# Where the low parts of streamed weights are made: VectorE's subtraction, or a negative from ScalarE and an adding DMA

## The chip, the cores and the metric

The kernel runs on one core of a Trainium2 chip. The metric is the time of the device, in microseconds (us), of one execution: the median of three executions of the kernel before is 1641.2 us (1640.48 to 1641.28).

The engines are named as the profile names them: PE is TensorE's matmul, PEld its weight load, DVE is VectorE, ACT is ScalarE, POOL is GpSimd, SP is SyncE. ACTq, POOLq and SPq are the queues from which these engines issue DMAs.

## The reference

The reference is a chain of two blocks on a sequence of 512 tokens with 1024 features, in float32. The first block projects the normed input by `w_in`, attends in chunks, convolves, gates and projects back. The second block has a layer with a sparse attention and a gated linear attention, a layer with stick-breaking attention, and behind each an MLP of width 4096. Nearly all of the arithmetic is the product of activations with weight matrices:

```
proj = jnp.einsum('bsd,de->bse', h, w_in[l])
...
def squared_relu_mlp(n, w_up, w_down):
    return jnp.square(jax.nn.relu(n @ w_up)) @ w_down
...
for layer in range(DEPTH_2):
    n = rmsnorm_2(h, g_mix[layer])
    ...
    h = h + squared_relu_mlp(rmsnorm_2(h, g_ffn[layer]), w_up[layer], w_down[layer])
```

## The kernel before

**Three products for one.** TensorE multiplies in a format that keeps fewer bits than float32 (float32r in the code). So every operand is split: `hi` is the value as that format keeps it, `lo` is what is left, and a product is made of three matmuls: hi by hi, lo by hi, hi by lo. For activations `split` makes the two parts, for weights that stream in from memory `split_w` (L161).

**A piece of weights.** The weights come through SyncE's queue into `raw` tiles (two buffers, 1 MB each as a rule, `load_raw`, L174). Half of a raw tile is a piece: 128 partitions by 1024 elements. For a piece `split_w` has ScalarE write `whi` as a copy (L170) and VectorE write `wlo` as raw minus whi (L171). `whi` and `wlo` have three buffers each, so a piece can be made while TensorE still uses the two before it. Both instructions are put ahead of other work by `first()`, a priority for the scheduler that orders each engine's queue.

**Who uses pieces.** `proj_fm` (L251) streams a matrix as 1024 rows by 128 columns, so its pieces are 128x8x128 (for matrices with 512 or 256 rows the columns grow); one piece serves one or two tiles of 512 tokens, 24 matmuls in all: per row block hi by hi (L246), lo by hi (L247), hi by lo (L248). The last matmul that reads a `whi` buffer is an L247, the last that reads a `wlo` an L248. `proj_tok` (L268) streams pieces of 128x2x512, also 24 matmuls (L282 to L284). There are 214 pieces. In the program 128 of the 208 that the change touches are 128x8x128, 20 are 128x4x256 and 60 are 128x2x512.

**Around them.** Attention runs beside the projections as generators (`weave`, `tick`), a step behind every few matmuls. In an MLP, eight pieces of `w_up` (six, and two of the next quarter) alternate with four calls of `down_pair`, which take their weights apart in another way (`weight_forms`, L1143): its own `put` stays as it is, and it uses the same three buffers of `whi` and `wlo`. GpSimd issues no DMA in this kernel; it adds squares (`SumSq`, L308), rotates queries and keys (`rope`, L645 to L647), and forms parts of the gated linear attention (`level`, L875 to L881). The order on each engine is the scheduler's; every engine takes its queue in order.

Of the kernel before, what the change touches and what calls it, by code (L numbers as in the profile page):

```python
# [8 lines left out]
F32 = mybir.dt.float32  # L9
# [3 lines left out]
AF = mybir.ActivationFunctionType  # L13
ALU = mybir.AluOpType
AX = mybir.AxisListType

P = 128
# [26 lines left out]
def body(tc, A, out, dbg=None):  # L44
    nc = tc.nc
    ACT, DVE, PE, POOL = nc.scalar, nc.vector, nc.tensor, nc.gpsimd

    with ExitStack() as es:
# [12 lines left out]
        def uid(s):  # L61
            cnt[0] += 1
            return f"{s}_{cnt[0]}"
# [94 lines left out]
            PE.matmul(ps, q[0], k[1], start=False, stop=False)  # L158
            PE.matmul(ps, q[1], k[0], start=False, stop=True)

        def split_w(raw, w, pieces=1):  # L161

            kd = raw.shape[1]
            hi = wp.tile([P, kd, w], F32R, tag="whi", bufs=3, name=uid("whi"))
            lo = wp.tile([P, kd, w], F32R, tag="wlo", bufs=3, name=uid("wlo"))
            n = kd // pieces
            for k in range(0, kd, n):
                ks = slice(k, k + n)
                with first():
                    ACT.activation(hi[:, ks, :], raw[:, ks, :], AF.Copy)  # L170
                    DVE.tensor_tensor(lo[:, ks, :], raw[:, ks, :], hi[:, ks, :].bitcast(F32), op=ALU.subtract)  # L171
            return hi, lo

        def load_raw(kd, w, *parts, pieces=1):  # L174
# [79 lines left out]
        def proj_fm(W, r0, c0, ncols, xs, evac):  # L254


            kd = len(xs)
            w = 1024 // kd
            for ch in range(0, ncols, 2 * w):
                cw = min(2 * w, ncols - ch)  # L260
                raw = load_raw(kd, cw, (0, W[r0:r0 + kd * P, c0 + ch:c0 + ch + cw]))
                for hf in range(0, cw, w):
                    hi, lo = split_w(raw[:, :, hf:hf + w], w)
                    for mt in range(0, w, P):
                        fm_tile(hi, lo, mt, xs, evac, (ch + hf + mt) // P)
                        yield

        def proj_tok(W, r0, c0, xs, evac, tts=range(NT), pieces=1):  # L268

            kd = len(xs)  # L270
            pss = {tt: psum("tk") for tt in tts}
            for k0 in range(0, kd, 4):
                raw = load_raw(4, 512, (0, W[r0 + k0 * P:r0 + (k0 + 4) * P, c0:c0 + 512]), pieces=pieces)
                for k2 in range(0, 4, 2):
                    hi, lo = split_w(raw[:, k2:k2 + 2, :], 512, 2 if pieces > 1 and k0 + k2 == 0 else 1)
                    for j in range(2):
                        k = k0 + k2 + j
                        for tt in tts:
                            xh = xs[k][0][:, tt * P:(tt + 1) * P]
                            xl = xs[k][1][:, tt * P:(tt + 1) * P]  # L280
                            ps = pss[tt]
                            PE.matmul(ps, xh, hi[:, j, :], start=k == 0, stop=False)  # L282
                            PE.matmul(ps, xh, lo[:, j, :], start=False, stop=False)  # L283
                            last = PE.matmul(ps, xl, hi[:, j, :], start=False, stop=k == kd - 1)  # L284
                            tick(last)
                    run_pending(last)
                    if k < kd - 1:
                        yield
            for tt in tts:
                with first():  # L290
                    evac(tt, pss[tt])
            yield
# [55 lines left out]
        r0 = cp.tile([P, NT], F32, name="r0")  # L348
# [39 lines left out]
        W = A["w_in"]  # L388
# [246 lines left out]
        W = A["w_in_ab"]  # L635
# [38 lines left out]
        raw = load_raw(KD, P, (0, W[:, 2048:2176]), (96, W[:, 3144:3160]))  # L674
# [597 lines left out]
        W = A["w_in_c"]  # L1272
# [171 lines left out]
```

## Time and profile before

| what | us |
|---|---|
| median of three executions | 1641.2 |
| the profiled execution | 1639.93 |
| its span, first to last instruction | 1638.2 |
| PE busy | 1601.4 |
| DVE busy | 1040.7 |
| ACT busy | 732.9 |
| POOL busy | 207.8 |

A matmul's record lasts longer than the step from one matmul to the next, since matmuls are pipelined: the step is read from the start times in the timeline, not from the mean of a group. Times are counted from the start of the span.

### The profile page before, as it was taken

Reading aid. Unit: us, or ns where it says so; the run is one execution under the profiler, and the core shown is the slowest. Engines: PE = TensorE matmul, PEld = TensorE weight load, DVE = VectorE, ACT = ScalarE, POOL = GpSimd, SP = SyncE. Lnnn points to the kernel's source line nnn. Section 1 sums busy time; section 2 is a strip of 40 time slices with the busy share of each in tenths; the row PEclk is TensorE's granted clock in tenths of the full one; section 3 lists DMA queues with packets and bytes.
Section 4 is the critical chain, followed back from the end, with each engine's and each line's share of the span. In section 5 each row is a group of like instructions: output and inputs, shape, how many; then the busy total and the mean of one; then the engine's idle time right before and its main releaser. Section 6 shows DMA issues by size and latency. Waiting matters only on the chain.

```text
span 1638.2 us, 21483 instructions
## 1 busy us (share of the span) xinstructions
PE 1601.4 (98%) x8440; PEld 1358.3 (83%) x8440; DVE 1040.7 (64%) x1887; ACT 732.9 (45%) x1172; POOL 207.8 (13%) x295
## 2 busy tenths in 40 slices
PE   9999999999998889999999999999999999999999
PEld 7887888888777667888989898888887789898987
DVE  5546443444658886568678795434557876877952
ACT  6343332225544535455554443334554554535341
POOL 3100000003322451210000000211213200000000
PEclk9999999999999999999999999999999999999999
DMA  6421123233222110223333322332121233333322
GB/s 203 150 77 52 52 77 118 88 104 115 79 78 77 52 52 26 71 85 103 104 103 104 103 89 92 103 99 82 52 78 52 77 103 104 103 104 103 104 77 77
DMA packets 129220, 146.39 MB, mean 89 GB/s; under 512 B 4048, under 2 KB 109152, under 8 KB 129120
## 3 DMA queue, kind: packets, MB, share of 16 engines
q1 hardware_dynamic: 122848, 141.11, 26.4%
q10 hardware_dynamic: 6272, 3.92, 0.8%
q8 instruction: 66, 1.08, 0.3%
q14 instruction: 34, 0.28, 0.0%
HBM read 142.92 MB, written 2.10 MB: 89 GB/s over the span
## 4 chain that ended last, share of the span: by engine, by line
PE 90%; DVE 4%; POOL 2%; ACT 1%; issue 1%; DMA 0%; POOLq 0%; DVEq 0%
PE fm L246 16%; PE fm L248 16%; PE fm L247 16%; PE tk L282 5%; PE tk L283 5%; PE tk L284 5%; PE sw L1195 5%; PE sw L1194 5%; PE sw L1193 5%; PE tr L331 3%; PE oc L1342 1%; PE S L1318 1%; PE S L469 1%; PE pa L493 1%; DVE wlo L171 1%
## 5 line engine op out<-in xcount | busy, mean ns | idle before, releaser
L246 PE MATMUL fm<-hi,whi 128*128 128x512 f32 x1224 | 484.2, 396 | 0.0
L247 PE MATMUL fm<-lo,whi 128*128 128x512 f32 x1224 | 477.5, 390 | 0.7 <-DVE lo L152 0.7
L248 PE MATMUL fm<-hi,wlo 128*128 128x512 f32 x1224 | 477.7, 390 | 0.0
L170 ACT ACTIVATE whi<-raw 128x1024 fp32r<-128x1024 f32 (+1 forms) x214 | 225.9, 1056 | 441.6 <-PE fm L247 286.8
L171 DVE TENSOR_TENSOR wlo<-raw,whi 128x1024 fp32r<-128x1024 f32 (+1 forms) x214 | 270.5, 1265 | 198.9 <-ACT whi L170 198.1
L248 PEld LDWEIGHTS fm<-hi,wlo 128*128 128x128 f32 x1224 | 229.8, 188 | 48.3
L247 PEld LDWEIGHTS fm<-lo,whi 128*128 128x128 f32 x1224 | 230.1, 188 | 47.8 <-DVE lo L152 2.0
L246 PEld LDWEIGHTS fm<-hi,whi 128*128 128x128 f32 x1224 | 230.0, 188 | 45.7 <-issue 0.5
L282 PE MATMUL tk<-whi,hi 128*128 128x512 f32 x472 | 196.6, 416 | 1.2 <-ACT va L795 0.6
L284 PE MATMUL tk<-whi,lo 128*128 128x512 f32 x472 | 187.3, 397 | 0.0
L283 PE MATMUL tk<-wlo,hi 128*128 128x512 f32 x472 | 186.8, 396 | 0.0
L308 POOL TENSOR_TENSOR ssq<-ssq,sq 128x512 f32<-128x512 f32 x25 | 38.6, 1553 | 557.6 <-ACT sq L306 557.3
L1195 PE MATMUL sw<-hi,wlo 128*128 128x256 f32 x384 | 108.7, 283 | 0.0
L1194 PE MATMUL sw<-lo,whi 128*128 128x256 f32 x384 | 108.7, 283 | 0.0
L1193 PE MATMUL sw<-hi,whi 128*128 128x256 f32 x384 | 108.6, 283 | 0.0
L284 PEld LDWEIGHTS tk<-whi,lo 128*128 128x128 f32 x472 | 89.9, 191 | 19.4
L282 PEld LDWEIGHTS tk<-whi,hi 128*128 128x128 f32 x472 | 90.8, 192 | 18.3 <-ACT vb L795 1.5
L283 PEld LDWEIGHTS tk<-wlo,hi 128*128 128x128 f32 x472 | 90.6, 192 | 15.5 <-DVE wlo L171 0.2
L1193 PE MATMUL sw<-hi,wh 128*128 128x256 f32 x288 | 81.5, 283 | 0.0
L1194 PE MATMUL sw<-lo,wh 128*128 128x256 f32 x288 | 81.5, 283 | 0.0
L1195 PE MATMUL sw<-hi,wl 128*128 128x256 f32 x288 | 81.5, 283 | 0.0
L1194 PEld LDWEIGHTS sw<-lo,whi 128*128 128x128 f32 x384 | 73.7, 192 | 0.2
(353 smaller groups left out, 2338.2 us busy)
## 6 DMA issues: line engine op xcount, KB each, us to landing
raw<-in_w_up SPq DMA_DIRECT2D x32, 1024.0 KB, 5.3
raw<-in_w_down SPq DMA_DIRECT2D x32, 1024.0 KB, 4.9
raw<-in_w_in SPq DMA_DIRECT2D x22, 1024.0 KB, 5.0
raw<-in_w_in_ab SPq DMA_DIRECT2D x14, 1024.0 KB, 4.9
raw<-in_w_in_c SPq DMA_DIRECT2D x12, 1024.0 KB, 4.9
raw<-in_w_out SPq DMA_DIRECT2D x4, 1024.0 KB, 5.0
raw<-in_w_out_ab SPq DMA_DIRECT2D x4, 1024.0 KB, 5.0
raw<-in_w_out_c SPq DMA_DIRECT2D x4, 1024.0 KB, 4.9
```

The source lines that it names most:

```text
L170: ACT.activation(hi[:, ks, :], raw[:, ks, :], AF.Copy)
L171: DVE.tensor_tensor(lo[:, ks, :], raw[:, ks, :], hi[:, ks, :].bitcast(F32), op=ALU.subtract)
L246: PE.matmul(ps, wh, xh, start=k == 0, stop=False)
L247: PE.matmul(ps, wh, xl, start=False, stop=False)
L248: last = PE.matmul(ps, wl, xh, start=False, stop=k == kd - 1)
L282: PE.matmul(ps, xh, hi[:, j, :], start=k == 0, stop=False)
L283: PE.matmul(ps, xh, lo[:, j, :], start=False, stop=False)
L284: last = PE.matmul(ps, xl, hi[:, j, :], start=False, stop=k == kd - 1)
L331: PE.transpose(ps[:, j * P:(j + 1) * P], s_, ident)
L1193: PE.matmul(half(ps, n % 2), wh, xh, start=j == 0, stop=False)
L1194: PE.matmul(half(ps, n % 2), wh, xl, start=False, stop=False)
L1195: last = PE.matmul(half(ps, n % 2), wl, xh, start=False, stop=j == 3)
```

## The change

For the pieces of `proj_fm`, and for those of `proj_tok` but its first call (which loads in four parts), VectorE's subtraction is left out. ScalarE writes `wlo` as the negative of `whi`, and GpSimd issues a DMA that adds the weights, read once more from memory, to `wlo` in place. `src` is the view of the matrix that the piece holds. The constant at the end is the number of bytes in each partition that are set aside for GpSimd's DMAs.

```diff
-        def split_w(raw, w, pieces=1):
+        def split_w(raw, w, pieces=1, src=None):
...
                 with first():
                     ACT.activation(hi[:, ks, :], raw[:, ks, :], AF.Copy)
-                    DVE.tensor_tensor(lo[:, ks, :], raw[:, ks, :], hi[:, ks, :].bitcast(F32), op=ALU.subtract)
+                    if src is None:
+                        DVE.tensor_tensor(lo[:, ks, :], raw[:, ks, :], hi[:, ks, :].bitcast(F32), op=ALU.subtract)
+                    else:
+                        ACT.activation(lo[:, ks, :], hi[:, ks, :].bitcast(F32), AF.Copy, scale=-1.0)
+                        nc.gpsimd.dma_start(lo[:, ks, :], src, accum_op=ALU.add)
...
                 for hf in range(0, cw, w):
-                    hi, lo = split_w(raw[:, :, hf:hf + w], w)
+                    src = W[r0:r0 + kd * P, c0 + ch + hf:c0 + ch + hf + w].rearrange("(k p) c -> p k c", p=P)
+                    hi, lo = split_w(raw[:, :, hf:hf + w], w, src=src)
...
                 for k2 in range(0, 4, 2):
-                    hi, lo = split_w(raw[:, k2:k2 + 2, :], 512, 2 if pieces > 1 and k0 + k2 == 0 else 1)
+                    ks_ = r0 + (k0 + k2) * P
+                    src = None if pieces > 1 else W[ks_:ks_ + 2 * P, c0:c0 + 512].rearrange("(k p) c -> p k c", p=P)
+                    hi, lo = split_w(raw[:, k2:k2 + 2, :], 512, 2 if pieces > 1 and k0 + k2 == 0 else 1, src)
...
-    nc = bacc.Bacc("TRN2", target_bir_lowering=False, num_devices=1, dynamic_dma_scratch_size=2048)
+    nc = bacc.Bacc("TRN2", target_bir_lowering=False, num_devices=1, dynamic_dma_scratch_size=4096)
```

The scheduler orders the queues anew. ScalarE's queue in the first quarter of the first MLP, before (`ha` is the hidden activation of a tile, `t3b` a scale made once):

```order
L170 ACTIVATE whi_6153<-raw_6151 128x1024
L324 ACTIVATE t3b_6035<-bc_6030 128x512
L1117 ACTIVATE ha_6037<-ha_6037 128x512
L1136 ACTIVATE hi_6049<-ha_6037 128x256
L1117 ACTIVATE ha_6040<-ha_6040 128x512
L148 ACTIVATE hi_6061<-ha_6040 128x512
```

and after, at the same place:

```order
L171 ACTIVATE whi_6253<-raw_6251 128x1024
L332 ACTIVATE t3b_6133<-bc_6128 128x512
L175 ACTIVATE wlo_6254<-whi_6253 128x1024
L1125 ACTIVATE ha_6135<-ha_6135 128x512
L1125 ACTIVATE ha_6138<-ha_6138 128x512
L1144 ACTIVATE hi_6147<-ha_6135 128x256
L148 ACTIVATE hi_6159<-ha_6138 128x512
```

The negative (L175) stands one place behind the copy here, with other work between the two; elsewhere it follows the copy directly. GpSimd's queue there before, where the sums of squares ahead of the first MLP are followed at once by those behind it:

```order
L308 TENSOR_TENSOR ssq_5761<-ssq_5761,sq_5851 128x512
L308 TENSOR_TENSOR ssq_5761<-ssq_5761,sq_5878 128x512
L308 TENSOR_TENSOR ssq_5761<-ssq_5761,sq_5899 128x512
L308 TENSOR_TENSOR ssq_8841<-ssq_8841,sq_8913 128x512
L308 TENSOR_TENSOR ssq_8841<-ssq_8841,sq_8952 128x512
```

and after:

```order
L176 DMA wlo_6049<-in_w_up 128x8x128
L316 TENSOR_TENSOR ssq_5853<-ssq_5853,sq_5973 128x512
L316 TENSOR_TENSOR ssq_5853<-ssq_5853,sq_5994 128x512
L176 DMA wlo_6099<-in_w_up 128x8x128
L176 DMA wlo_6166<-in_w_up 128x8x128
L176 DMA wlo_6199<-in_w_up 128x8x128
L176 DMA wlo_6254<-in_w_up 128x8x128
L176 DMA wlo_6287<-in_w_up 128x8x128
```

Where nothing stood, the 40 DMAs of this MLP now stand in a row. GpSimd's queue in the attention of the second block, where it rotates the queries, before:

```order
L875 TENSOR_TENSOR dl_4557<-Bc_3498 128x512
L878 TENSOR_TENSOR dl_4557<-dl_4557,kb_3685 128x128x2
L875 TENSOR_TENSOR dl_4610<-Bc_3566 128x512
L645 TENSOR_TENSOR rp_4342<-qa_4304,ropeQ 128x128
L646 TENSOR_TENSOR rp_4343<-qa_4304,ropeQ 128x128
L647 TENSOR_TENSOR qa_4304<-rp_4342,rp_4343 128x4x32
```

and after:

```order
L883 TENSOR_TENSOR dl_4636<-Bc_3563 128x512
L176 DMA wlo_4654<-in_w_in_ab 128x2x512
L886 TENSOR_TENSOR dl_4636<-dl_4636,kb_3752 128x128x2
L883 TENSOR_TENSOR dl_4690<-Bc_3631 128x512
L653 TENSOR_TENSOR rp_4418<-qa_4380,ropeQ 128x128
L654 TENSOR_TENSOR rp_4419<-qa_4380,ropeQ 128x128
L176 DMA wlo_4737<-in_w_in_ab 128x2x512
L655 TENSOR_TENSOR qa_4380<-rp_4418,rp_4419 128x4x32
```

Two DMAs have come in between, one of them between two steps of a rotation.

## Rows read from the trace of the kernel before

**Rows 1.** The page's first part: busy us, share of the span, instructions
```profile
PE 1601.4 (98%) x8440; PEld 1358.3 (83%) x8440; DVE 1040.7 (64%) x1887; ACT 732.9 (45%) x1172; POOL 207.8 (13%) x295
```
**Rows 2.** Costliest groups: instruction, count, busy us, mean ns, idle before it by releaser
```profile
L170 ACT ACTIVATE whi<-raw 128x1024 fp32r<-128x1024 f32 (+1 forms) x214 | 225.9, 1056 | 441.6 <-PE fm L247 286.8
L171 DVE TENSOR_TENSOR wlo<-raw,whi 128x1024 fp32r<-128x1024 f32 (+1 forms) x214 | 270.5, 1265 | 198.9 <-ACT whi L170 198.1
...
L308 POOL TENSOR_TENSOR ssq<-ssq,sq 128x512 f32<-128x512 f32 x25 | 38.6, 1553 | 557.6 <-ACT sq L306 557.3
```
**Rows 3.** Timeline in the second MLP: start, us, engine, instruction, idle before it
```profile
1402.83 1.06 ACT L170 ACTIVATE whi<-raw 128x1024 fp32r<-128x1024 f32 x1 [0.92 <-PE fm L247]
...
1403.80 0.62 ACT L1117 ACTIVATE ha<-ha 128x512 f32<-128x512 f32 x1
...
1403.93 1.23 DVE L171 TENSOR_TENSOR wlo<-raw,whi 128x1024 fp32r<-128x1024 f32 x1 [0.18 <-ACT whi L170]
...
1408.27 1.06 ACT L170 ACTIVATE whi<-raw 128x1024 fp32r<-128x1024 f32 x1 [3.40 <-PE fm L247]
```
**Rows 4.** Instructions of line L170 alone, by stretch: length, ACT busy (count), clock, DMA
```profile
33.00:77.00 44.00, 9.22 (x9) 1.00 0.55 169
77.00:191.00 114.00, 12.98 (x13) 1.00 0.18 58
191.00:412.00 221.00, 42.45 (x40) 1.00 0.31 98
```
**Rows 5.** Timeline, ScalarE alone, between two quarters of the first MLP
```profile
802.57 1.06 ACT L170 ACTIVATE whi<-raw 128x1024 fp32r<-128x1024 f32 x1 [0.26 <-PE sw L1194]
...
812.64 1.06 ACT L170 ACTIVATE whi<-raw 128x1024 fp32r<-128x1024 f32 x1 [0.72 <-PE sw L1194]
820.88 1.06 ACT L170 ACTIVATE whi<-raw 128x1024 fp32r<-128x1024 f32 x1 [6.66 <-PE fm L247]
```
**Rows 6.** DMA issues: count, KB each, median us from issue to landing
```profile
raw<-in_w_up SPq DMA_DIRECT2D x32, 1024.0 KB, 5.3
...
raw<-in_w_in_ab SPq DMA_DIRECT2D x1, 512.0 KB, 3.4
raw<-in_w_in_ab SPq DMA_DIRECT2D x1, 64.0 KB, 2.2
```
**Rows 7.** Instructions on the tile raw: ns min/median/max, first and last start
```profile
L171 DVE TENSOR_TENSOR wlo<-raw,whi x214: 691/1225/7231, 6.6 to 1619.3; 128x1024 fp32r<-128x1024 f32 x106, 128x512 fp32r<-128x512 f32 x1
L180 SPq DMA_DIRECT2D raw<-in_w_up x32: 367/368/368, 692.5 to 1551.0; - x32
```
**Rows 8.** Busy us by stretch: PE, PEld, DVE, ACT, POOL, granted clock, DMA share, GB/s
```profile
500.00:600.00 100.00, 84.00 (x394) 67.70 (x392) 89.49 (x192) 43.34 (x81) 50.79 (x64) 0.93 0.16 53
...
1300.00:1540.00 240.00, 240.00 (x1481) 217.03 (x1480) 185.78 (x300) 116.36 (x175) 0.00 (x0) 1.00 0.31 101
```
**Rows 9.** Chain that ended last, 500 to 620 us, shares by line
```profile
by line: DVE wlo L171 9.8%; DVE isc L786 8.2%; issue 7.1%; DVE m L785 6.7%; PE tk L282 5.7%; PE gr L887 5.7%; PE tk L283 5.2%; PE tk L284 5.2%; POOL rp L646 4.0%; POOL dl L875 3.6%; POOL dl L878 3.5%; POOL rp L645 2.9%; POOL qa L647 2.8%; P
```
**Rows 10.** PE's waits, 500 to 660 us: waiting line, releaser, us, times, longest
```profile
PE tr L331 <- POOL qa L647: 5.4, 3, 2.5
PE gr L887 <- DVE m L982: 4.8, 1, 4.8
```
**Rows 11.** Busy us in four short stretches, columns as in Rows 8
```profile
520.00:524.00 4.00, 0.66 (x2) 0.28 (x2) 3.90 (x8) 0.06 (x1) 3.79 (x7) 0.88 0.00 0
...
560.00:564.00 4.00, 4.00 (x11) 3.13 (x11) 2.40 (x2) 1.41 (x3) 2.15 (x3) 0.50 0.56 216
```

## The prediction

> **What bounds the kernel now.** I read the busy times first: PE is busy 98% of the span, DVE 64%, ACT 45%, POOL 13% [rows 1]. So TensorE sets the end almost everywhere, and work taken off VectorE is worth something only where PE waits. The groups come next: the line that goes away, DVE L171, is 214 instructions and 270.5 us busy, and before it VectorE idles 198.9 us, mostly for ScalarE's copy; ScalarE itself idles 441.6 us before its copies, 286.8 of them until PE releases a buffer [rows 2]. So pieces are made as soon as a buffer comes free, and then lie ready. The timeline gives the pace: one copy starts at 1402.83 and the next at 1408.27, so TensorE takes 5.44 us over a piece, and in this stage, 240 us long, PE is busy all 240 at the full clock [rows 3, 8]. Since there are three buffers, the low part of a piece may land two paces, 10.9 us, after its buffer came free (and some 0.45 us more, as the third matmul is the first to read it). Today it takes 1.06 + 0.18 for the copy and 1.23 for the subtraction, about 2.5 us [rows 3]: there are 8 us to spare in latency, and VectorE is used 1.23 us of each 5.44.
>
> The one place where DVE bounds is 500 to 600 us: DVE busy 89.5, PE only 84.0 [rows 8], and the chain that ended last runs through DVE L171 for 9.8% of those 120 us, 11.8 us [rows 9].
>
> **What the change removes.** 208 subtractions, 208 x 1.265 = 263 us of VectorE. Where PE never waits for VectorE that is worth nothing. In 500 to 620 us it is worth at most the 11.8 us of the chain. But there GpSimd is on the chain too (about 17% in the POOL lines shown, and PE waits 5.4 us for its rotated queries [rows 9, 10]), and some 13 DMAs are put into its queue, two of them around a rotation. At a quarter of the issue time G below (a 128x2x512 piece has 256 rows, not 1024), 0.6 us each, that is 8 us, of which I put half on the chain. Sum for this stretch: -11.8 + 4 = -8 us; bounds -12 and, if each of these DMAs makes the queue wait another 3 us for its buffer, +35. One VectorE instruction of the kind removed was held for 7.23 us [rows 7]; that one is in this stretch and within the 11.8.
>
> **What it adds on ScalarE.** 208 negatives of 1.06 us, 220 us. They hide in the 441.6 us of idle before the copies [rows 2]; ScalarE's share goes from 45% to 58%. At the paced stages one such instruction and an L1117 of 0.62 us [rows 3] come ahead of the DMA: copy 1.06, 0.62 at times, negative 1.06, two semaphores of 0.18, so 3.0 us from the free buffer to the DMA. Without the cover it would cost that only in latency, of which there is enough.
>
> **What it adds on SyncE's queue.** Nothing is added; raw buffers are released by ScalarE's copy, 1.4 us sooner. Free.
>
> **What it adds on GpSimd and the DMA engines.** This decides. For each 128x8x128 piece, GpSimd must issue a transfer of 1024 rows of 512 B, and the engines must read the row of memory, read the row of the tile, and write the sum. Two prices, both absent from the trace:
>
> G, the issue. Lower end: SyncE's queue issues a 1 MB load in 0.37 us [rows 7]. Upper end: GpSimd works out every one of the three accesses of 1024 rows by itself at the rate at which it goes through a tile, 1553 ns for 512 elements [rows 2], 3.03 ns each: 3072 x 3.03 = 9.3 us. Nearest is a GpSimd instruction over a whole tile: one over 512 elements is 1.55 us, over the 1024 of a piece it would be twice that; I take the middle of 1.55 and 3.1, G = 2.3 us.
>
> D, from issue to landing. The plain load of exactly this shape (1024 rows of 512 B) lands in 3.4 us, and 1024 rows of 64 B in 2.2 us [rows 6]. So about 2.2 us are fixed and 1.2 us pay for the other 448 KB. The tile's own 512 KB are read as well, 1.4 us more: 4.8 to 5.0 us, near the 5.3 us of a 1 MB load [rows 6]. In the MLP the raw loads keep the engines 31% busy [rows 8], so the 2.8 us of data stretch to 2.8 / 0.69 = 4.1: D = 6.3 us. Ends: 3.4 (the second read is free) and 14 (the sum runs at a third of the rate: 2.2 + 3 x 4.1).
>
> In latency, 3.0 + 2.3 + 6.3 = 11.6 us against 11.3: a single piece would be about in time. In rate it depends on whether two such transfers can be under way at once. No row shows it. With overlap the rate is that of the dearer part, below 5.44 us; one at a time, a piece takes P = G + D = 8.6 us against TensorE's 5.44. I take one at a time: the room set aside for GpSimd's DMAs is 4096 bytes a partition, and each transfer puts 192 accesses on each of 16 engines, 21 bytes for an access when one is under way and 10 when two are, hardly more than an address.
>
> The Trainium skill supports this choice, and no run here shows it. DMA: Bandwidth & Descriptors (Terms) gives a descriptor 16 B, and Collectives: The Full Stack (The bandwidth ceiling) says that an adding transfer needs two reads for each write. By the two pages the reads of one piece take 129 entries of 256 in an engine's ring, and two pieces do not fit.
>
> **The sum.** Each charged piece costs 8.6 - 5.44 = 3.16 us. Which are charged:
> - 33 to 77 us: 9 copies in 44 us, the fast pace; together with the first of the next stretch, 10 pieces.
> - 77 to 191 us: 13 in 114 us, 8.8 us each [rows 4], slower than P: none.
> - 191 to 412 us: 40 in 221 us, 5.5 each [rows 4]. Eight of them are 128x4x256 (half the rows, issued ahead while TensorE takes its 5.44 us), and behind each pause the three buffers hold pieces. Going through the sequence: 8 charged, then three times 3, then 3 and the last 7 less what the gaps give: 23.
> - The MLPs: between two quarters TensorE works 40 us on `down_pair`, and three copies (802.57 to 812.64) are made before it ends [rows 5]. So of a run of n the first four are free. The runs are 10, 8, 8, 14 and 10, 8, 8, 6: 6 + 4 + 4 + 10 + 6 + 4 + 4 + 2 = 40.
> - The 60 pieces of 128x2x512: a quarter of the rows and a slower pace by the attention beside them: none.
>
> 73 pieces x 3.16 = 231 us. With the -8 of the attention: 1639.9 + 231 - 8 = 1863, and as the median stands 1.3 us above the profiled execution, **1864 us**.
>
> **The clock.** After 520 to 524 us, where PE was busy 0.66 of 4 us, the granted clock was 0.50, the lower level, and at that level 11 matmuls went in 4 us [rows 11]: 24 would take 8.7 us. Waits of 3 us a piece may bring it down. But 8.7 is about P, so a piece at the low clock is no later than its low part; only behind a pause a few us are lost, within the range.
>
> **The rivals.**
> 1. *Hidden* (the other side). Transfers overlap, or P stays under 5.44 one at a time: with the lower ends it is 0.37 + 3.4 = 3.8 us. For it: one queue has several loads of SyncE in flight, and the latency fits. Then only the attention's -8 is left (at most -12, at worst nothing): 1632 us. It decides below P = 5.8. Against it: the second read, and busy engines. The Trainium skill has a rule for it: DMA: Bandwidth & Descriptors (Anatomy of one DMA) puts a GpSimd DMA at 2.0 us plus bytes / 436e3, an estimate of 3.2 us for a piece, and by that it would be hidden even one at a time.
> 2. *Issue in software* (dearer). GpSimd goes row by row: G = 9.3, P = 15.6. Then each of the 73 costs 10.2 (745 us), the 13 of 77 to 191 us cost 6.8 each (88), and about half of the first pieces of a run, 10 in all, are late as well (100): 1640 + 933 = 2573 us. A slow sum in the engines (D = 14) gives P = 16.3 and about the same. For it: POOL's 3.03 ns a step; against: that is a rate for arithmetic. Half way lies P = 11 to 12: 1640 + 85 x 6 = 2150.
> 3. That the change does not do what it says: the order has the 208 DMAs and has lost the 208 subtractions, so I give it nothing.
>
> **Chances.** One at a time with P between 6.4 and 11: 0.62. Dearer than that: 0.27. Hidden: 0.11, of which 0.07 faster by over 0.2% (which is about what a measurement of this kernel can tell from no change), 0.03 within, 0.01 slower. The range leaves out the hidden case and the dear end: from P = 6.4 (73 x 0.96 = 70 less 8: 1702) to between P = 12 and 15.6 (2380).
>
> **What would show it.** DVE L171 shrinks from 214 to 6 and DVE's share to under 50%. PE's wait is for the DMA of `wlo`, at L248 and at L283, and it comes in the MLPs and at 191 to 412 us; PE busy there is two thirds. The copies stand 8 to 9 us apart instead of 5.44. In 77 to 191 us and in the `down_pair` stretches nothing changes. I am wrong if the DMAs of `wlo` overlap, if POOL's issue of one is over 4 us or under 1, or if the queue of POOL, not the transfer, holds PE in the attention.

## The result, and the profile after

The changed kernel takes 1858.13 us (median of four executions, 1840.18 to 1859.66) against 1640.84 us for the kernel before beside it: a ratio of 1.1305, 95% interval 1.1271 to 1.1339. It is slower by 217 us; the forecast was 1864 us.

The profiled execution took 1859.66 us, with a span of 1858.0 us where before had 1638.2. Busy time of each engine, share of the span and instructions (before: [rows 1]):

```profile
PE 1671.9 (90%) x8440; PEld 1388.0 (75%) x8440; DVE 814.7 (44%) x1679; ACT 925.2 (50%) x1380; POOL 477.4 (26%) x503
```

VectorE lost its 208 instructions and 226 us, ScalarE gained 208 and 192 us, GpSimd gained 208, which are the transfers. None of them is near full. PE has the same 8440 matmuls, is busy 70 us longer, and waits far more. The groups say for what (columns as in [rows 2]; L253 is the matmul that L248 was, L171 and L175 are ScalarE's copy and its negative, L176 is the issue of a transfer):

```profile
L253 PE MATMUL fm<-hi,wlo 128*128 128x512 f32 x1224 | 507.8, 415 | 152.5 <-DMA wlo<-in_w_up 84.3
...
L171 ACT ACTIVATE whi<-raw 128x1024 fp32r<-128x1024 f32 (+1 forms) x214 | 225.8, 1055 | 499.9 <-PE fm L252 411.6
...
L176 POOL DMA_DIRECT2D wlo<-in_w_up x64 | 100.1, 1564 | 598.1 <-DVE xT L1213 262.4
L175 ACT ACTIVATE wlo<-whi 128x1024 fp32r<-128x1024 f32 x208 | 218.8, 1052 | 3.8 <-DVE bias L462 1.4
```

All of the new idle time of PE, 152.5 us, stands before L253, the first matmul that reads `wlo`. PE's waits, grouped by what ended them (us in all, times, longest), name the transfer each time, and the `proj_tok` pieces (L291) hardly at all:

```profile
PE fm L253 <- DMA wlo<-in_w_up: 84.3, 42, 4.5
PE fm L253 <- DMA wlo<-in_w_in: 47.2, 17, 8.1
PE fm L253 <- DMA wlo<-in_w_down: 13.1, 5, 3.9
PE fm L253 <- DMA wlo<-in_w_out: 7.8, 5, 2.5
...
PE tk L291 <- DMA wlo<-in_w_in_ab: 1.0, 1, 1.0
```

How one run of pieces goes is seen in the second MLP. First GpSimd's timeline (start, duration, what it waited before it), then PE's first matmuls on two low parts:

```profile
1558.47 1.56 POOL L176 DMA_DIRECT2D wlo<-in_w_up  x1 [41.31 <-DVE xT L1213]
1565.67 1.57 POOL L176 DMA_DIRECT2D wlo<-in_w_up  x1 [5.64 <-ACT wlo L175]
1573.12 1.56 POOL L176 DMA_DIRECT2D wlo<-in_w_up  x1 [5.88 <-issue]
1581.26 1.57 POOL L176 DMA_DIRECT2D wlo<-in_w_up  x1 [6.58 <-ACT ha L1125]
1588.45 1.56 POOL L176 DMA_DIRECT2D wlo<-in_w_up  x1 [5.62 <-ACT ha L1125]
...
1610.12 1.57 POOL L176 DMA_DIRECT2D wlo<-in_w_up  x1 [5.93 <-DVE wlo L1165]
```

```profile
1580.99 0.50 PE L253 MATMUL fm<-hi,wlo 128*128 128x512 f32 x1 [0.67 <-DMA wlo<-in_w_up]
...
1588.18 0.50 PE L253 MATMUL fm<-hi,wlo 128*128 128x512 f32 x1 [1.46 <-DMA wlo<-in_w_up]
```

A low part lands and PE reads it at 1580.99; 0.27 us later, at 1581.26, GpSimd issues the next. The same at 1588.18 and 1588.45. The second issue of the run, at 1565.67, does wait for ScalarE, whose negative for it ends at 1565.27. From the third on, the releaser that the trace names (an activation on ScalarE, or "issue") changes from row to row and was done long before: the negative for the issue of 1581.26 ends at 1576.77. Only the landing stands at a fixed distance. So one transfer of such a piece is under way at a time, and the pace is 0.27 + 1.57 for the issue + 5.4 for the rest, 7.2 to 7.4 us, where PE needs 5.44. From the second issue to the eighth, 1565.67 to 1610.12, it is 44.45 / 6 = 7.41 us.

Smaller transfers do overlap in the same kernel. A piece of `w_att_out` has 512 rows. Behind one of `w_in`, with 1024, it is issued at once:

```profile
294.33 1.57 POOL L176 DMA_DIRECT2D wlo<-in_w_in  x1 [5.58 <-ACT ga L573]
295.22 2.01 POOL L176 DMA_DIRECT2D wlo<-in_w_att_out  x1
```

```profile
301.68 0.50 PE L253 MATMUL fm<-hi,wlo 128*128 128x512 f32 x1 [1.89 <-DMA wlo<-in_w_in]
```

The second issue is over at 297.23, and the first transfer lands only at 301.68. What is limited is not the number of transfers.

The issue itself counts in the landing (count, KB each, median us from issue to landing; before: [rows 6]):

```profile
raw<-in_w_up SPq DMA_DIRECT2D x32, 1024.0 KB, 5.4
wlo<-in_w_up POOLq DMA_DIRECT2D x64, 512.0 KB, 7.1
```

Where the time came in is read from the start of the same ScalarE copy (the 25th, 67th, 103rd, 151st, 175th and 211th piece, the two halves of the first counted as one) in two traces. The table gives how much later than in the kernel before it starts, in us, for the changed kernel and for the experiments below:

| piece starts before at | after | two_in_flight | lo_last | filler | plain_copy | act_dve | tok_only | ab_only |
|---|---|---|---|---|---|---|---|---|
| 159.0 | 35.9 | 9.9 | 19.2 | 35.9 | 4.7 | 0.0 | 0.1 | 0.3 |
| 410.2 (projections) | 81.9 | 13.4 | 46.8 | 87.1 | 4.6 | -0.1 | 0.1 | 0.2 |
| 713.9 (attention) | 77.9 | 7.2 | 42.2 | 83.7 | -6.9 | -5.1 | -4.7 | -4.2 |
| 1099.5 (first MLP) | 159.0 | 15.2 | 119.3 | 151.2 | -6.9 | -5.0 | -4.3 | -4.2 |
| 1285.3 | 159.7 | 15.9 | 120.2 | 151.9 | -6.6 | -2.4 | -3.5 | -4.2 |
| 1607.3 (second MLP) | 219.6 | 31.1 | 178.9 | 212.3 | -5.9 | -3.3 | -3.3 | -4.2 |

### The profile page after: what moved, and what is told of

Its sections match the earlier page's. It is cut to its first block, busy times and chain, and to the rows that moved or that the text cites. A ratio compares the mean times of both kernels' runs of the same rounds, so it can differ in the third digit from the quotient of the medians.

```text
span 1858.0 us, 22001 instructions
## 1 busy us (share of the span) xinstructions
PE 1671.9 (90%) x8440; PEld 1388.0 (75%) x8440; DVE 814.7 (44%) x1679; ACT 925.2 (50%) x1380; POOL 477.4 (26%) x503
## 5 line engine op out<-in xcount | busy, mean ns | idle before, releaser
L253 PE MATMUL fm<-hi,wlo 128*128 128x512 f32 x1224 | 507.8, 415 | 152.5 <-DMA wlo<-in_w_up 84.3
L251 PE MATMUL fm<-hi,whi 128*128 128x512 f32 x1224 | 504.6, 412 | 0.0
L252 PE MATMUL fm<-lo,whi 128*128 128x512 f32 x1224 | 497.0, 406 | 0.0
L171 ACT ACTIVATE whi<-raw 128x1024 fp32r<-128x1024 f32 (+1 forms) x214 | 225.8, 1055 | 499.9 <-PE fm L252 411.6
L253 PEld LDWEIGHTS fm<-hi,wlo 128*128 128x128 f32 x1224 | 242.5, 198 | 234.3 <-DMA wlo<-in_w_up 103.1
L252 PEld LDWEIGHTS fm<-lo,whi 128*128 128x128 f32 x1224 | 242.0, 198 | 51.4 <-issue 0.5
L251 PEld LDWEIGHTS fm<-hi,whi 128*128 128x128 f32 x1224 | 242.9, 198 | 47.4 <-issue 0.5
L176 POOL DMA_DIRECT2D wlo<-in_w_up x64 | 100.1, 1564 | 598.1 <-DVE xT L1213 262.4
L175 ACT ACTIVATE wlo<-whi 128x1024 fp32r<-128x1024 f32 x208 | 218.8, 1052 | 3.8 <-DVE bias L462 1.4
L291 PE MATMUL tk<-wlo,hi 128*128 128x512 f32 x472 | 186.6, 395 | 1.0 <-DMA wlo<-in_w_in_ab 1.0
L176 POOL DMA_DIRECT2D wlo<-in_w_in x44 | 69.0, 1569 | 267.6 <-issue 105.9
L291 PEld LDWEIGHTS tk<-wlo,hi 128*128 128x128 f32 x472 | 90.1, 191 | 16.9 <-DMA wlo<-in_w_in_ab 1.5
```

Source lines behind the costliest of these rows:

```text
L175: ACT.activation(lo[:, ks, :], hi[:, ks, :].bitcast(F32), AF.Copy, scale=-1.0)
L176: nc.gpsimd.dma_start(lo[:, ks, :], src, accum_op=ALU.add)
L251: PE.matmul(ps, wh, xh, start=k == 0, stop=False)
L252: PE.matmul(ps, wh, xl, start=False, stop=False)
L253: last = PE.matmul(ps, wl, xh, start=False, stop=k == kd - 1)
```

## The experiments

Two theories stood against each other. *One at a time*: the issue and the transfer of a piece stand in a row, since GpSimd does not begin the next before the last has landed, for want of room for its descriptors. *Full engines*: the DMA engines have more to do for a piece than fits in 5.44 us, and the order changes nothing.

**Room for two: two_in_flight.** The space for descriptors grows by half; a buffer of the attention's scores pays for it.

```diff
-SLOTS = {..., "Ss": 4, ...}
+SLOTS = {..., "Ss": 3, ...}
...
-dynamic_dma_scratch_size=4096
+dynamic_dma_scratch_size=6144
```

> As the changed kernel, but the scratch space for descriptors on POOL's queue is 6144 B instead of 4096 B (paid for with one buffer less of the tag Ss, 3 instead of 4), so that the descriptors of two accumulating transfers fit instead of one. Theory 'one at a time' (the pace of 7.2 to 7.8 us is POOL's issue of 1.57 us plus 0.27 us plus a transfer of about 5.4 us, in a row, because the next issue finds no room): the issue now lies beside the transfer before it, the pace falls to 5.4 to 5.7 us against PE's 5.44 us, most of the 219 us go, and the time is 1635 to 1680 us. Rival 'full engines' (64 packets of 83 ns on each of 16 engines are 5.3 us, and half of a raw load, 32 packets of 57 ns, adds 1.8 us: 7.1 us a piece whatever the order): the pace stays at 7.0 to 7.3 us, and the time at 1810 to 1858 us.

It took 1671.6 us (ratio to before 1.0188, 1.0173 to 1.0204). Some 186 of the 217 us are gone by a change of one size. GpSimd's timeline shows a run in the second MLP:

```profile
1506.10 1.56 POOL L176 DMA_DIRECT2D wlo<-in_w_up  x1 [6.68 <-ACT hi L1144]
1511.54 1.55 POOL L176 DMA_DIRECT2D wlo<-in_w_up  x1 [3.88 <-ACT wlo L175]
1516.98 1.57 POOL L176 DMA_DIRECT2D wlo<-in_w_up  x1 [3.89 <-ACT hi L1144]
```

In the middle of the run the issues stand 5.44 us apart, TensorE's own pace, although the landing still takes 7.3 us from the issue (median of `wlo<-in_w_up`). Each transfer is as slow as it was; two are under way. PE's waits for `w_up`'s low parts fall from 84.3 to 14.7 us. *One at a time* holds.

The stretch 220 to 400 us shows why the rival's sum failed (busy us of PE, PEld, DVE, ACT and POOL, granted clock, share of the DMA engines, GB/s; first the changed kernel, then this one):

```profile
220.00:400.00 180.00, 161.00 (x688) 130.06 (x687) 31.55 (x46) 73.78 (x90) 44.32 (x30) 0.94 0.81 149
```

```profile
220.00:400.00 180.00, 178.38 (x800) 146.32 (x799) 36.50 (x53) 89.34 (x111) 54.08 (x37) 1.00 1.01 189
```

PE is busy 178.38 of 180 us at a DMA share of 1.01. The rival added up packet durations as if an engine could have one packet at a time, and a share over 1 shows that they overlap; their sum is no bound on the pace.

**Smaller transfers in the same room: halves.**

```diff
-nc.gpsimd.dma_start(lo[:, ks, :], src, accum_op=ALU.add)
+h2 = kd // 2
+for kk in (0, h2):
+    nc.gpsimd.dma_start(lo[:, kk:kk + h2, :], src[:, kk:kk + h2, :], accum_op=ALU.add)
```

> As the changed kernel, but each accumulating transfer is issued as two, of half the rows each (64 KB x 4 instead of 512 KB in one for the pieces of 8 row blocks), so that the descriptors of three halves fit in the same 4096 B. POOL's issue of a half is 1.2 to 1.3 us by the rows of 256 to 512 packets, 2.4 to 2.6 us a piece. Theory 'one at a time': the issue of the next half lies beside the transfer of the one before, the pace is that of the transfers alone, 5.4 to 5.7 us, and the time 1635 to 1690 us. Rival 'full engines': 7.0 to 7.3 us, 1810 to 1860 us. If each half has a fixed cost of its own that nothing hides (landing of 5.6 us at the least, one after another), the pace rises to 8 us and more, and the time to over 1900 us.

It took 1683.61 us (1.0254, 1.0223 to 1.0285). The room is that of the changed kernel, and yet most of the loss is gone; two kernels that have only the overlap in common agree to 12 us. GpSimd's issues of `w_up` (count, busy, mean ns, idle before them) and their landings:

```profile
L178 POOL DMA_DIRECT2D wlo<-in_w_up x128 | 166.5, 1501 | 442.5 <-DVE xT L1215 214.6
```

```profile
wlo<-in_w_up POOLq DMA_DIRECT2D x128, 256.0 KB, 6.1
```

Half a transfer is issued in 1.50 us and lands after 6.1, against 1.56 and 7.1 for a whole one. Other halves are under way beside it, so how much of either goes with the size stays open. The expectation's 1.2 to 1.3 us for the issue was too low.

**Without the adding: plain_copy.**

```diff
-nc.gpsimd.dma_start(lo[:, ks, :], src, accum_op=ALU.add)
+nc.gpsimd.dma_start(lo[:, ks, :], src)
```

> As the changed kernel, but the transfer on POOL's queue copies the weights instead of adding them: the adding is left out, so the low parts are the weights themselves. It reads one source instead of two, and has 65 descriptors to read where it had 129. Both theories: packets of about 57 ns as on SP's queue, 64 of them on each engine are 3.6 us, with 1.8 us of raw load 5.4 us, and two transfers fit; a pace at or under PE's 5.44 us and a time of 1632 to 1660 us. If the time stays above 1800 us, the software queue is slow by itself and not the adding.

It took 1634.12 us (0.9961, 0.9947 to 0.9976). The issue and the landing:

```profile
L176 POOL DMA_DIRECT2D wlo<-in_w_up x64 | 56.2, 878 | 518.3 <-DVE xT L1213 254.8
```

```profile
wlo<-in_w_up POOLq DMA_DIRECT2D x64, 512.0 KB, 4.8
```

Reading the tile as well and adding costs 0.68 us in the issue (1.56 against 0.88) and 2.3 us to the landing (7.1 against 4.8). The software queue alone does not make the kernel slow.

**Every second piece: alternate.**

```diff
-hi, lo = split_w(raw[:, :, hf:hf + w], w, src=src)
+hi, lo = split_w(raw[:, :, hf:hf + w], w, src=src if hf else None)
```

> As the changed kernel, but of the pieces of proj_fm only every second (the second half of each raw load) takes its low part by the accumulating transfer; the first half goes through VectorE's subtraction as before the change. The pieces of proj_tok stay on the transfer. PE takes 10.9 us for two pieces, one transfer takes 7.2 to 7.8 us and its issue included is always done in that time. Theory 'pace': no wait is left in the MLPs and the projections at 191 to 410 us, only the first pieces after a cold start pay; 1630 to 1650 us, PE's clock back over 0.99. Rival 'latency' (each transfer has to be waited for whatever its neighbours do, since the low part is needed 7 us after the raw load): half of the 219 us stays, about 1745 us.

It took 1647.21 us (1.0042, 1.0026 to 1.0057). Two pieces of PE are 10.9 us, a transfer 7.2, and PE's waits for low parts are all but gone:

```profile
PE fm L253 <- DMA wlo<-in_w_in: 3.6, 1, 3.6
PE fm L253 <- DMA wlo<-in_w_up: 3.5, 1, 3.5
PE tk L291 <- DMA wlo<-in_w_in_ab: 1.1, 1, 1.1
```

It is the pace that is charged, not each transfer's latency.

**The low part needed later: lo_last.** The matmuls of the high part come first in each tile.

```diff
     PE.matmul(ps, wh, xh, start=k == 0, stop=False)
-    PE.matmul(ps, wh, xl, start=False, stop=False)
-    last = PE.matmul(ps, wl, xh, start=False, stop=k == kd - 1)
-    tick(last)
+    tick(PE.matmul(ps, wh, xl, start=False, stop=False))
+for k in range(kd):
+    last = PE.matmul(ps, lo[:, k, mt:mt + P], xs[k][0], start=False, stop=k == kd - 1)
```

> As the changed kernel, but in each tile of proj_fm the 8 matmuls with the low part of the weights come after the 16 with the high part, instead of every third: the low part is needed 3.2 us later in each piece of w = 128 (16 matmuls of 0.227 us are 3.6 us, where the first of three stood at 0.45 us). Theory 'the transfers set the pace': the wait comes 3.2 us later once for each of the stretches in which the transfers fall behind (some 10 to 12 of them: one or two at 20 to 186 us and at 191 to 410 us, four groups in each MLP), 30 to 38 us in all, 1815 to 1835 us; within a stretch the issues stay 7.2 us and more apart. Rival 'latency': each piece waits for its own transfer, and the 3.2 us count in each of some 75 charged pieces, which pay 1.8 to 3 us each: nearly all of the 219 us go, 1640 to 1680 us.

It took 1817.2 us (1.1095, 1.1063 to 1.1127). The size is that of the pace, and the rival, 1640 to 1680, falls. Not all of it is as expected, though: by the table 35 of the 41 us come before 410 us, 17 of them in the first stretch, and the two MLPs together give 5 where eight groups were to give 26. Of the 58 gaps that follow an issue of `w_up` within a run, 20 are over 8.5 us (1558.76 to 1567.99, for one), against 7 of 58 in the changed kernel. In each of these 27 gaps about a whole raw load, 0.96 to 1.06 MB, moved on SyncE's queue. Why the loads hit more often here is open.

**PE kept busy: filler.** PE was busy 70 us longer in the changed kernel, because behind a pause its granted clock fell to the lower of its two levels, 0.50. Around a wait of 4.01 us that ended at 829.64, the stretch 828 to 832 us of the changed kernel reads (columns as above):

```profile
828.00:832.00 4.00, 2.36 (x6) 1.87 (x7) 1.89 (x3) 1.08 (x3) 1.57 (x1) 0.50 0.30 38
```

Whether that costs anything of its own is tested by matmuls that fill the pause.

```diff
 def fm_tile(hi, lo, mt, xs, evac, i, extra=0):
     kd = len(xs)
     ps = psum("fm")
+    for r in range(extra):
+        PE.matmul(ps, hi[:, r, mt:mt + P], xs[r][0], start=True, stop=True)
```

`extra` is 6 in the three calls of `proj_fm` with `Wu` and 0 elsewhere.

> As the changed kernel, but in the MLPs' first projections (w_up, 64 pieces) PE begins each piece with 6 more matmuls of 0.227 us whose sums are overwritten: 1.36 us of work ahead of the first matmul that needs the low part, so that PE waits less and its clock is kept up. Theory 'the transfers set the pace': a piece is 7.2 us and more apart whatever PE does in it, 6.8 us of work fit, PE's waits and the low clock are two ways to spend the same time; the time rises only by 1.4 us at the end of each of the 8 groups or so, 1850 to 1875 us, while the waits for w_up's low parts fall from 131 us to under 80 us and the mean granted clock rises from 0.961 to over 0.97. Rival 'the clock costs by itself': the 70 us by which PE was busy longer than before come on top of the transfers; w_up's part of them, some 35 us, is saved, and the time falls to 1815 to 1840 us.

It took 1848.25 us (1.1266, 1.124 to 1.1292). Busy times, the added matmuls, and the waits for `w_up`:

```profile
PE 1733.2 (94%) x8824; PEld 1447.4 (78%) x8824; DVE 816.0 (44%) x1679; ACT 927.2 (50%) x1380; POOL 477.4 (26%) x503
```

```profile
L249 PE MATMUL fm<-hi,whi 128*128 128x512 f32 x384 | 98.1, 391 | 0.0
```

```profile
PE fm L255 <- DMA wlo<-in_w_up: 14.7, 14, 2.7
```

384 more matmuls, 87 us at 0.227 each, and the time is not higher: they fit into pauses. It is 10 us lower, but the two intervals overlap (the changed kernel's is 1.1271 to 1.1339), and one execution of the changed kernel, at a mean granted clock of 0.973, took 1840.18 us where the other three, at 0.961 to 0.965, took 1856.62 to 1859.66. (The expectation's 131 us of waits took those for `w_in` along; `w_up`'s alone were 84.3.) The mean granted clock rose from 0.961 to 0.975. The 10 us lie 2 us below the range of the transfers' pace and 8 us above that of the clock; by the table the first MLP became 13.6 us shorter (67.5 for 81.1 us of delay) and the second did not change (60.4 for 59.9). If the fillers themselves cost the 1.4 us at the end of each of 8 runs that the expectation gave them, the clock's own cost in `w_up` was up to 21 us; this is an estimate, and with the 1% by which executions of the changed kernel differ it may be less. Most of the 70 us is time in which the transfer was not there yet anyway. The projections were not tested.

Where the lower clock does cost can be read in the trace of the changed kernel: at the end of a run, where no further transfer is waited for. The last low part of the run shown above:

```profile
1620.06 0.80 PE L253 MATMUL fm<-hi,wlo 128*128 128x512 f32 x1 [4.47 <-DMA wlo<-in_w_up]
1620.66 0.63 PE L251 MATMUL fm<-hi,whi 128*128 128x512 f32 x1
1621.08 0.63 PE L252 MATMUL fm<-lo,whi 128*128 128x512 f32 x1
...
1623.95 0.39 PE L251 MATMUL fm<-hi,whi 128*128 128x512 f32 x1
1624.18 0.39 PE L252 MATMUL fm<-lo,whi 128*128 128x512 f32 x1
```

The matmuls first start 0.43 us apart, then 0.23. Until 1623.22 that loses 1.6 us, and nothing behind takes it back. Five of the eight runs of `w_up` end like this, at 1.6 to 2.9 us each, some 11 us in all.

**ScalarE's part alone: act_dve.**

```diff
-nc.gpsimd.dma_start(lo[:, ks, :], src, accum_op=ALU.add)
+DVE.tensor_tensor(lo[:, ks, :], raw[:, ks, :], lo[:, ks, :].bitcast(F32), op=ALU.add)
```

> As the changed kernel without its transfers: ScalarE still writes the negative of the high part (208 more instructions of 1.06 us), and VectorE adds the weights to it from the buffer they were loaded into, so that VectorE has as many instructions as before the change. It prices ScalarE's part by itself. Theory 'hidden': ScalarE has room for 220 us more; the low part is ready 1.06 us later, against three buffers of 5.44 us; 1639 to 1645 us. Rival 'ScalarE is late': the instructions stand ahead of the work that frees PSUM and of the attention's exponentials on ScalarE, and the loss shows in the attention and the MLPs; 1655 us and more.

It took 1637.52 us (0.9985, 0.9976 to 0.9995), a little faster than expected. The 208 negatives of ScalarE are free. The gain comes between 491 and 714 us, where pieces start 1.2 us late and then 5.1 early, and VectorE has all its 1887 instructions.

**Only where it is free: tok_only and ab_only.**

```diff
 # tok_only, in proj_fm
-hi, lo = split_w(raw[:, :, hf:hf + w], w, src=src)
+hi, lo = split_w(raw[:, :, hf:hf + w], w)
...
 # ab_only, in proj_fm and in proj_tok alike
+src = ... if W is A["w_in_ab"] else None
```

> As the changed kernel, but only the pieces of proj_tok (72 of 208) take their low part by the accumulating transfer; all pieces of proj_fm go through VectorE's subtraction, as before the change. Theory 'pace of the piece': the pieces of proj_tok cost nothing, since they do not come closer together than 7.2 us for longer than the three buffers last, or PE takes 8 us and more for them there; what is left is the relief of VectorE in the attention (the plain copy stood 11 us lower after the stretch 480 to 680 us than before it): 1629 to 1637 us. Rival 'each transfer costs': 72 of 208 pieces carry a third of the 219 us, about 1710 us. Rival 'the relief came from proj_fm': 1641 us, no change.

> As the changed kernel, but only the 28 pieces of w_in_ab (proj_tok and proj_fm alike, at about 430 to 720 us of the span, where PE waits for VectorE) take their low part by the accumulating transfer; all others go through VectorE's subtraction, as before the change. Theory 'relief of VectorE in the attention': the stretch gains what it gained in the changed kernel (85.5 to 77.9 us behind, 7.6 us) and nothing is lost elsewhere: 1630 to 1636 us, faster than the kernel with only proj_tok on the transfer. Rival 'order': the planner lays VectorE's and ScalarE's work in the attention out anew whenever the split changes, which gave 5 us even where ScalarE's negative came on top and VectorE kept all its work: 1635 to 1639 us.

In tok_only 56 pieces use the transfer, by the issues in its trace; the expectation's 72 is a miscount. tok_only took 1637.11 us (0.9983, 0.9974 to 0.9992) and ab_only 1636.46 us (0.9977, 0.9969 to 0.9986). The pieces of `proj_tok` are free, and both kernels are faster than before by more than the uncertainty, but by 3 us, not 7. ab_only is the fastest that computes the whole. Its time lies in the range of the rival 'order', and by the gain alone it cannot be told from act_dve.

**Is it VectorE's relief? ab_dve_kept and before_ss3.** ab_dve_kept leaves VectorE's subtraction in the 28 pieces of ab_only.

```diff
 else:
+    DVE.tensor_tensor(lo[:, ks, :], raw[:, ks, :], hi[:, ks, :].bitcast(F32), op=ALU.subtract)
     ACT.activation(lo[:, ks, :], hi[:, ks, :].bitcast(F32), AF.Copy, scale=-1.0)
```

> As the kernel with only w_in_ab's 28 pieces on the transfer, but in these pieces VectorE still makes its subtraction into the same tile, before ScalarE overwrites it with the negative of the high part: VectorE has as many instructions as before the change, and the transfer is 1.23 us later. Theory 'relief of VectorE': the gain of some 7 us goes, 1638 to 1645 us. Rival 'order': the gain does not hang on VectorE's work, and the time stays within 1.5 us of the kernel without the subtraction.

It took 1656.2 us (1.0098, 1.0084 to 1.0111), 20 us more than ab_only and more than either theory gave. It doesn't decide: ScalarE's negative now has to wait for VectorE, and what is queued behind it on ScalarE comes later too. ScalarE's largest wait between 410 and 740 us, and PE's:

```profile
ACT wlo L176 <- DVE wlo L175: 31.8, 18, 4.7
```

```profile
PE fm L254 <- DMA wlo<-in_w_in_ab: 6.3, 1, 6.3
```

9.5 us of the loss are there by the piece that starts at 447 us, ahead of the stretch in question, and 4.2 come between 491 and 714 us, where ab_only gains 6.9. That the waits on ScalarE make up the loss is argued, not tested.

before_ss3 changes no work, only the layout of VectorE's queue in the attention, and is the control for the buffer that two_in_flight gave up.

```diff
-SLOTS = {..., "Ss": 4, ...}
+SLOTS = {..., "Ss": 3, ...}
```

> The kernel before the change, with one buffer less of the tag Ss (3 instead of 4) and nothing else: all 214 subtractions stay on VectorE, no transfer is added, but the planner lays some of VectorE's work in the attention out in another order. It is the control for the kernels with two and three transfers in flight, which gave up that buffer, and for the gain of 4 to 5 us in the attention that three kernels showed, one of them without any relief of VectorE. Theory 'order': any new layout moves the attention by some us, 2 to 6 us in either sign: 1634 to 1638 or 1642 to 1646 us. Rival 'the order is worth nothing, the gain needs the split changed': within 1 us of before, 1639 to 1641 us.

It took 1639.89 us (0.9999, 0.999 to 1.0008). The buffer costs nothing, and this layout is worth nothing.

**Room for three: three_in_flight.**

```diff
-SLOTS = {..., "go": 8, "Ss": 4, ...}
+SLOTS = {..., "go": 7, "Ss": 3, ...}
...
-dynamic_dma_scratch_size=4096
+dynamic_dma_scratch_size=8192
```

> As the changed kernel, but with 8192 B for descriptors, so that three accumulating transfers fit (paid for with one buffer less of the tags Ss and go). It tells what the last 31 us of the kernel with two (1671.6 us) are. Theory 'full engines': with two in flight the engines were already busy for 1.00 of the stretches 60 to 110 and 220 to 400 us, so a third only queues behind them: 1665 to 1676 us. Rival 'still the issue': the first two transfers of each group of w_up stand 7.2 us apart even with two, and a third takes that away: 1645 to 1660 us.

It took 1673.15 us (1.0209, 1.0193 to 1.0225), the same as with two. The stretch 60 to 110 us (columns as above), with two and with three:

```profile
60.00:110.00 50.00, 45.82 (x216) 37.67 (x217) 6.63 (x39) 26.53 (x47) 11.41 (x8) 1.00 1.00 187
```

```profile
60.00:110.00 50.00, 46.90 (x211) 38.61 (x210) 6.63 (x39) 26.53 (x47) 11.19 (x8) 0.93 0.99 179
```

The share is 1.00 and 0.99, at 187 and 179 GB/s. The first two issues of a run of `w_up` are 7.2 us apart as before, but that distance is not the queue's: in the kernel before, ScalarE's first two copies of such a run stand as far apart, between them a wait for `down_pair`'s matmuls on PE (the first is in [rows 5], at 802.57):

```profile
809.76 1.06 ACT L170 ACTIVATE whi<-raw 128x1024 fp32r<-128x1024 f32 x1 [0.72 <-PE sw L1194]
```

Room is no longer the limit. What the last 31 us are stays open. That the engines are full is what the shares suggest, and plain_copy, which moves one read less, has none of the 31 us; but its issue is shorter too, and no run took the engines' load away alone.

## Why the prediction was right, and where its numbers were not

*What bounds.* Right. PE's pace of 5.44 us is the measure, and with the transfers faster than that (plain_copy, alternate) or overlapping (two_in_flight), the loss goes.

*One at a time.* This was the choice on which everything hung, made without a row, and the runs show it twice: by more room and by smaller transfers. The Trainium skill had supported it (DMA: Bandwidth & Descriptors, Terms, and Collectives: The Full Stack, The bandwidth ceiling): worked out from the two pages, a piece takes an estimated 129 entries of 256. By the same estimate 6144 B are 384 entries, room for two at 258, and two_in_flight agrees, with 5.44 us between issues.

*The issue G.* 1.57 us measured against 2.3. The lower end of the range from which it was taken, one instruction of 1.55 us, came close, but no run shows that the two are related: without the adding the issue is 0.88 us.

*The landing D.* 5.4 us behind the issue, and 0.27 to the next, against 6.3. The second read came out near its price: behind the issue the adding transfer takes 1.6 us more than the plain copy (7.1 - 1.56 against 4.8 - 0.88), against 1.4. What was wrong is the stretching by the raw loads, which I gave to every piece: some gaps are longer by that and more, most by little (below). P was 7.2 us and up, in place of 8.6. (Two sums of the prediction are rounded down: to the DMA it is 3.1 us and not 3.0, and the dear end 14.5 and not 14. Nothing hangs on either.) The Trainium skill's estimate of 3.2 us (DMA: Bandwidth & Descriptors, Anatomy of one DMA) was less than half of the 7.1 us measured from issue to landing; by it the change would have been hidden even one at a time, and the measurement decides.

*The stretch by a raw load.* In the first run of the first MLP, GpSimd's issues at 813.10 and 829.91 us follow 8.8 and 9.9 us behind the ones before, those at 804.32 and 820.02 only 7.2 and 6.9. SyncE's timeline has the two raw loads of that time in one row, the first issued at 803.72 and the second ending its issue 17.28 us later, at 821.0; each falls into one of the long gaps:

```profile
803.72 17.28 SPq L185 DMA_DIRECT2D raw<-in_w_up  x2
```

The first long gap and the short one behind it, 804.00 to 813.00 and 813.00 to 820.00 us, differ in what the engines move (columns as above):

```profile
804.00:813.00 9.00, 6.40 (x30) 5.00 (x30) 3.68 (x15) 4.67 (x8) 1.56 (x1) 1.00 0.88 175
```

```profile
813.00:820.00 7.00, 7.00 (x24) 5.55 (x24) 3.15 (x8) 2.09 (x4) 1.57 (x1) 0.76 0.63 77
```

A load beside the transfer is not enough for a long gap, though: between the issues at 1588.45 and 1595.60, only 7.15 us apart, 1.00 MB moved on SyncE's queue as well. What makes the difference is open.

*The charged pieces.* Here two errors cancelled. I had the first four pieces of a run free in the MLPs. In the run shown above PE begins its first piece at 1568.80, only 10.3 us after the first issue, and the third piece already waits (1580.99). PE's waits from 1560 to 1625 us are six:

```profile
PE fm L253 <- DMA wlo<-in_w_up: 11.1, 6, 4.5
```

So two are free, and six of eight are charged: 11.1 us of waits, where I had four times 3.16, 12.6. Five of the six waits are 0.67 to 1.75 us, up to about the excess of the pace, 7.41 - 5.44 = 1.97; the last is 4.47, since its transfer, issued at 1610.12, lands only at 1620.06. In all, PE's 8 pieces last from 1568.80 to 1626.68, where `down_pair` goes on: 57.88 us, 14.4 more than eight times 5.44. Of the 3.3 us beside the waits the lower clock behind the last one takes 1.6; the rest lies at the edges of the six waits, where a matmul's record (0.39 us) outlasts its step (0.23).

By stage, the sum said 32 us to 191 us, 73 to 412, 76 in the first MLP and 51 in the second; the table gives 35.9, 46.0, 81.1 and 59.9. The term that was mis-sized most is the 73. Its count of 23 pieces fits the starts of the copies, its price does not: the delay grows by 18.5 us where 8 were charged, by 16.8 where three times 3 were, and by 10.7 where the last 6 were, some 2.0 us a piece and not 3.16. The MLPs came out near, and a little above, because a smaller excess fell on more pieces, with long gaps and the end of the run on top. That the total came within 6 us of 1864 is luck to that extent; the mechanism is not.

*The attention, -8 us.* The number held: between 491 and 714 us the changed kernel goes from 85.5 to 77.9 us late, 7.6 us. The reason may not. act_dve, which takes nothing off VectorE, gains 6.3 us in the same place (1.2 late to 5.1 early), tok_only 5.9 and ab_only 6.9; plain_copy gains 11.2. Busy times from 410 to 740 us, before, act_dve and ab_only in this order:

```profile
410.00:740.00 330.00, 301.91 (x1473) 246.71 (x1472) 239.27 (x533) 156.93 (x281) 106.64 (x131) 0.97 0.20 65
```

```profile
410.00:740.00 330.00, 307.79 (x1496) 251.69 (x1495) 237.67 (x539) 198.49 (x325) 103.04 (x131) 0.96 0.21 68
```

```profile
410.00:740.00 330.00, 307.21 (x1493) 250.48 (x1492) 216.17 (x511) 184.07 (x310) 125.37 (x158) 0.96 0.50 111
```

PE gets through about 20 matmuls more in both, with VectorE busy as long as before in one and 23 us less in the other. What brings these 6 us stays open: ab_dve_kept was spoilt by ScalarE's wait, and before_ss3 shows only that another layout of VectorE's queue isn't enough by itself. The +4 in the sum rested on 0.6 us for an issue of 256 rows; tok_only's took 1.20 to 1.21 us. The feared +35, GpSimd's queue holding up the attention, did not come.

*The clock.* Right in kind: the mean granted clock fell (0.994 to 0.961), and filler shows that most of the time it takes is time in which PE would have waited. "A few us" was too little: some 11 us are lost at the ends of `w_up`'s runs, and up to some 20 is the estimate from filler.

*ScalarE and the slow stretches.* Right: act_dve shows the negatives to be free, PE waits 1.0 us in all for the low parts of `proj_tok`, the delay does not move between 1099.5 and 1285.3 us (159.0 to 159.7), and from the piece at 96.5 us (36.1) to that at 170.9 (35.9) it doesn't grow either. It did grow from 25.8 us at the piece of 76.3 to that point, so the first slow pieces still paid for those before them.

*The rivals.* Hidden fell with P at 7.2, above its limit of 5.8; plain_copy shows the time it would have had, 1634 us against the 1632 given. Issue in software fell with an issue of 1.57 us. Of what would show it, three things came otherwise. The copies stand 7 to 10 us apart, not 8 to 9. PE was not down to two thirds in the charged stretches: from 220 to 400 us it was busy 161.00 of 180, 89%. And it hardly waited at the matmul that was L283 (1.0 us).

## What to carry to other kernels

A buffer's depth covers latency only; ask of each new transfer whether its issue and landing together fit into the consumer's pace when one has to end before the next begins, and if not, whether two can be under way, since the room for descriptors may decide it. Look for that in the timeline of the issuing engine: here, an issue that followed each landing at the same small distance, whatever releaser was named, was a queue with room for one. And count the busy time that a lower clock adds only after asking whether the engine would have waited there anyway; here it told at the end of a run, where no wait followed.

## What the runs showed of the hardware that was not expected

- An adding transfer of 512 KB from GpSimd's queue: 1.56 us of issue and 7.1 us from its start to the landing; the same without the adding 0.88 and 4.8; half of it with the adding, others beside it, 1.50 and 6.1.
- The next issue began 0.27 us after the landing when there was room for one (4096 B), and 5.44 us after the last issue when there was room for two (6144 B); a third place (8192 B) brought nothing (1673.15 us against 1671.6). With 4096 B a transfer of 512 rows was issued while one of 1024 was under way.
- The DMA share of a stretch goes over 1 (1.01 here): packet durations overlap, and a sum of them is not the time that an engine needs.
